# Two-layer hybrid encoder on one core: another order of work around the feed-forward part, down projection in chunks of 3, 4, 4 pairs

## Chip, cores, metric

The kernel runs on 1 core of one Trainium2 chip. The metric is the time of one execution on the device, in microseconds (us); of several runs the median is given.

## What is computed

The reference runs two layers over x (1 x 1024 x 1024, float32). Each layer mixes tokens (attention, a spatial gate and a short convolution side by side) and then applies a convolutional gated feed-forward part, which is where the change lies:

```python
h = _rmsnorm(x, norm1_g[l]); p = h @ w_in[l]
...
x = x + mix @ w_out[l]
h2 = _rmsnorm(x, norm2_g[l])
up = _dwconv3(h2 @ ffn_w_up[l], ffn_conv_w[l])      # 1024 -> 5632, 3 taps along the sequence
gate, val = jnp.split(up, 2, axis=-1)               # 2816 each
x = x + (jax.nn.silu(gate) * val) @ ffn_w_down[l]   # 2816 -> 1024
```

## The kernel before

One core goes through the layers one after the other. A layer is: norm1 and the input projection; attention with the spatial gate and the convolution woven in; the output projection (`out_proj`, matmuls of lines 132 to 134); norm2 (`norm_a`, line 229, and `norm2_b`, transposes of line 679); the up projection in NFF = 22 tiles (`up_tile`); and the down projection (`down_chunk`). The order of instructions on each engine is set by the framework's scheduler, which simulates a time line of its own and takes, per engine, what it thinks ready; only inside `manual_schedule` does an engine keep the order in which the code is written, and before the change that is done for TensorE during attention alone.

Float32 matmuls are done as three: every operand is split into a rounded high half and the remainder, the low half (`split`: ScalarE copies the high half, line 108; VectorE or GpSimd subtracts it, line 119, as a letter `v` or `p` says). A product a x b is then high x high, high x low, low x high.

Both projections of the feed-forward part use a scheme with seven products of half-size blocks instead of eight (with sums of blocks as operands).

- **Up projection.** The operands on the activation side, named 11, 12, S1 to S4 and 22, are made once per layer at the end of norm2. `norm2_b` forms them per block of 128 rows (lines 695 to 698: VectorE and GpSimd), and `norm2_end` splits S1 to S4 when all blocks are there. On the weight side each tile f loads 2 x 512 KB (`up_load`, line 729), forms T1 to T4 on GpSimd (`up_prep`, line 745) and splits all seven (`up_split`). A tile is 7 products of 12 matmuls of 128x512 (`block_mm`, line 768) into PSUM banks named pa, po and pf. VectorE adds them up (line 796) and ScalarE copies the rest (line 797), a depthwise convolution of 3 taps follows for value and gate (`conv3`: one step on ScalarE, line 352, two on VectorE, lines 353 and 357), in two double banks named `big`; then the gate: tanh (line 822), lines 823 and 828 or 831 on VectorE. After every second tile four sums of blocks are formed (line 838) and the pair's seven operands are stored to DRAM (`gdram`, lines 829 and 841). Two tiles' first two products are started early, during norm2 (`up_ahead`).
- **Down projection.** 11 pairs of tiles, in CHUNKS = (2, 3, 3, 3) pairs. A chunk runs over the seven products m = 0 to 6; for each pair the operands are loaded from `gdram` (line 884), the weights (loaded at line 864) are subtracted on GpSimd where the product wants it (line 877), and both are split (`down_split`) into a ring of DRING slots. The matmuls (line 920) go to four banks: those with even m accumulate in two `big` double banks over the whole chunk, those with odd m go to pa, pa, po, pf. VectorE adds the banks into x (line 930), at each m. With 12 matmuls per pair and product there are 11 x 7 x 12 = 924 per layer.

PSUM has two `big` (two banks each), two pa, one po and one pf: all eight banks. SBUF is cut into named slots (H0 to H5, E0 to E9, W0 to W5, G0 to G7, Z0, Z1); a slot can be refilled when all that reads it is done. H0 and H1 hold x in the down projection. The program's `run` (from line 946) sets the order: norm2 blocks in a loop from line 1015, the tiles from line 1030, the chunks from line 1042. Three lines say what sets the places of PSUM:

```python
U, G = [self.big(), self.big()], {}                     # line 904
banks = [U[h][:, lo], U[h][:, hi]]                      # m even, line 912
banks = [self.acc(k) for k in (("pa", "pa"), ("po", "pf"))[h]]   # m odd, line 914
```

Of the kernel before, what the change touches and what calls it, by code (L numbers as in the profile page):

```python
# [11 lines left out]
ALU = mybir.AluOpType  # L12
# [21 lines left out]
CHUNKS = (2, 3, 3, 3)  # L34
DW = (("E3", "E4", "E8", "W3"), ("H4", "E3", "E4"), ("H2", "E8", "W3"), ("H4", "E3", "E4"))
DA = ("H3", "H5")
DRING = (
    "W1", "W4", "Z0", "Z1", "G0", "G2", "G3", "W2", "E0", "E1", "E2", "E5", "E6", "E7", "E9",
    "G6", "G7", "W0", "W5", "G4", "G1", "G5",
)  # L40
D_LO = "vvp"
D_T = "p"
D_SUM = "vvvv"
UPRING = ("E0", "E1", "E2", "E5", "E6", "E7", "E9", "G6", "G7")
# [11 lines left out]
CWE = ("p", "p")  # L56


class Trunk:
# [657 lines left out]

    def a_op(self, n, k):
# [19 lines left out]

    def up_prep(self, f, raws, B):


        b11, b21, b12, b22 = raws

        def sub(out, a, b):
            self.nc.gpsimd.tensor_tensor(out=out, in0=a, in1=b, op=ALU.subtract)  # L745

        if not B:
            B["11"] = self.up_split(b11, "v")
        sub(b11, b12, b11)
        B["T1"] = self.up_split(b11)  # L750
        sub(b11, b22, b11)
        B["T2"] = self.up_split(b11, "v")
        if "21" not in B:
            B["21"] = self.up_split(b21)
        sub(b12, b22, b12)
        B["T3"] = self.up_split(b12, "v")
        B["22"] = self.up_split(b22)
        sub(b21, b21, b11)
        B["T4"] = self.up_split(b21)
# [13 lines left out]
    def up_ahead(self, f, raws):  # L773

        B = {"11": self.up_split(raws[0], "v"), "21": self.up_split(raws[1], "v")}
        u, c2 = self.acc("pa"), self.acc(("po", "pf")[f])
        self.block_mm(u, "11", B["11"], True, False)
        self.block_mm(c2, "12", B["21"], True, True)
        if f == 0:
# [3 lines left out]
        return B, u, c2, p1  # L783

    def up_tile(self, f, B, ahead=None):
# [315 lines left out]
```

## Time and profile before

| | |
|---|---|
| median of 3 runs | 2300.79 us (2300.1 to 2304.73) |
| the profiled execution | 2304.89 us, its span 2303.1 us |
| TensorE (PE): busy, instructions | 2222.9 us (97%), 10564 |
| VectorE (DVE) | 1657.6 us (72%), 2123 |
| ScalarE (ACT) | 1121.1 us (49%), 2009 |
| GpSimd (POOL) | 1287.6 us (56%), 1133 |
| mean granted TensorE clock | 0.984 |

The profile is one execution on the chip. Busy is the time in which an engine has an instruction; "idle before" is the time for which it had none, with the instruction whose end released it. The granted clock is 1 at TensorE's higher level (2.4 GHz) and about 0.5 at its lower one (1.2 GHz). A layer ends at about 1154 us (layer 0) and 2297 us (layer 1).

### The profile page before, as it was taken

What the parts mean: (1) busy time and instruction counts of PE and PEld (TensorE: products, weight loads), DVE (VectorE), ACT (ScalarE), POOL (GpSimd) and SP (SyncE); (2) the same over time, 40 slices, a digit from 0 to 9 for tenths busy, and PEclk for the clock granted to TensorE, in tenths of its full rate; (3) what the DMA queues carried; (4) which work ended last, traced back from release to release, by engine and by line L of the source; (5) the groups of instructions that cost most, each with busy time, mean ns of one, the idle gap of its engine ahead of it and who ended that gap; (6) DMA issues with size and microseconds to landing.
All of it is one profiled execution on the core that took longest, in us unless ns stands there. A gap on an engine that the chain in (4) does not pass through costs nothing.

```text
span 2303.1 us, 29303 instructions
## 1 busy us (share of the span) xinstructions
PE 2222.9 (97%) x10564; PEld 1840.9 (80%) x10564; DVE 1657.6 (72%) x2123; ACT 1121.1 (49%) x2009; POOL 1287.6 (56%) x1133
## 2 busy tenths in 40 slices
PE   7999999989999999799999999999899999988998
PEld 6887887868888888588878878878688888876887
DVE  5468887276777777988645688862767777779885
ACT  4246776354544444443242467754545444444431
POOL 5463335685555554776454533356765555556761
PEclk9999999999999999899999999999899999999999
DMA  5000003222232325843230000041223333357431
GB/s 183 23 28 10 10 10 95 98 83 87 92 115 92 115 92 175 304 156 106 67 122 6 28 10 10 10 163 48 74 87 101 110 105 105 105 190 268 152 96 74
DMA packets 166852, 218.97 MB, mean 95 GB/s; under 512 B 11799, under 2 KB 117811, under 8 KB 166707
## 3 DMA queue, kind: packets, MB, share of 16 engines
q1 hardware_dynamic: 166706, 217.10, 28.3%
q8 instruction: 83, 1.36, 0.2%
q14 instruction: 63, 0.51, 0.1%
HBM read 159.92 MB, written 57.15 MB: 94 GB/s over the span
## 4 chain that ended last, share of the span: by engine, by line
PE 89%; DVE 4%; POOL 2%; DMA 2%; ACT 1%; issue 1%; SPq 0%; DVEq 0%; POOLq 0%; ACTq 0%
PE pa L768 20%; PE big L920 10%; PE pf L768 9%; PE pf L266 5%; PE po L768 5%; PE pa L536 5%; PE pa L920 3%; PE pa L134 3%; PE pa L133 3%; PE big L520 3%; PE big L519 3%; PE pa L132 3%; PE po L548 2%; PE po L549 2%; PE pf L920 2%; PE po L920 2%
## 5 line engine op out<-in xcount | busy, mean ns | idle before, releaser
L528 POOL TENSOR_SCALAR H<-H,rv 128x1024 f32<-128x1024 f32 x128 | 144.8, 1131 | 272.2 <-DVE rv L527 272.2
L119 POOL TENSOR_TENSOR E<-E,E 128x512 fp32r<-128x512 f32 (+1 forms) x123 | 167.6, 1364 | 172.7 <-ACT E L108 172.2
L108 ACT ACTIVATE E<-E 128x512 fp32r<-128x512 f32 (+1 forms) x227 | 141.6, 629 | 182.0 <-POOL E L745 69.3
L768 PE MATMUL pa<-H,E 128*128 128x512 f32 x840 | 210.8, 395 | 12.3 <-DVE H L796 12.3
L541 DVE TENSOR_TENSOR E<-pa,E 128x512 fp32r<-128x512 f32 x256 | 173.4, 688 | 49.6 <-ACT E L540 48.2
L768 PEld LDWEIGHTS pa<-H,E 128*128 128x128 f32 x840 | 160.0, 191 | 46.7 <-DVE H L796 13.2
L540 ACT ACTIVATE E<-pa 128x512 fp32r<-128x512 f32 x256 | 152.9, 597 | 90.4 <-PE pa L536 89.2
L536 PEld LDWEIGHTS pa<-ident,H 128*128 128x128 f32 x1024 | 128.0, 141 | 42.8 <-issue 5.1
L536 PE MATMUL pa<-ident,H 128*128 128x128 f32 x1024 | 154.9, 274 | 6.6 <-DVE E L541 6.6
L522 DVE TENSOR_REDUCE nm<-big 128x1 f32<-128x1024 f32 x128 | 155.7, 1216 | 6.7 <-PE big L520 6.6
L353 DVE SCALAR_TENSOR_TENSOR big<-H,cst,big 128x1023 f32<-128x1023 f32 x44 | 56.6, 1287 | 143.8 <-ACT big L352 143.8
L797 ACT ACTIVATE H<-pa 128x512 f32<-128x512 f32 x128 | 76.0, 594 | 164.0 <-PE pa L768 148.0
L525 ACT ACTIVATE H<-big,nm 128x1024 f32<-128x1024 f32 x128 | 142.4, 1112 | 17.7 <-DVE nm L522 17.6
L119 DVE TENSOR_TENSOR E<-E,E 128x512 fp32r<-128x512 f32 (+1 forms) x109 | 117.9, 1084 | 24.1 <-ACT E L108 24.1
L266 PE MATMUL pf<-H,G 128*128 128x512 f32 x320 | 130.7, 429 | 2.7 <-DVE Z L394 2.7
L768 PE MATMUL pa<-W,E 128*128 128x512 f32 x340 | 119.2, 400 | 12.7 <-ACT W L108 12.7
L108 ACT ACTIVATE G<-E 128x512 fp32r<-128x512 f32 (+2 forms) x126 | 68.6, 556 | 106.1 <-PE pa L133 21.0
L745 POOL TENSOR_TENSOR E<-E 128x512 f32<-128x512 f32 x66 | 103.1, 1563 | 4.4
L768 PE MATMUL po<-H,E 128*128 128x512 f32 x408 | 104.6, 389 | 0.0
L548 PE MATMUL po<-E,E 128*128 128x512 f32 x256 | 101.5, 396 | 2.1 <-DVE E L564 2.1
L108 ACT ACTIVATE G<-H 128x512 fp32r<-128x512 f32 (+1 forms) x94 | 58.5, 649 | 90.7 <-PE big L920 43.7
L549 PE MATMUL po<-E,E 128*128 128x512 f32 x256 | 101.3, 396 | 0.0
(430 smaller groups left out, 6554.1 us busy)
## 6 DMA issues: line engine op xcount, KB each, us to landing
E<-in_ffn_w_up_dram SPq DMA_DIRECT2D x66, 512.0 KB
gdram<-H SPq DMA_DIRECT2D x66, 512.0 KB
H<-gdram SPq DMA_DIRECT2D x66, 512.0 KB
out_dram<-H SPq DMA_DIRECT2D x32, 512.0 KB
E<-in_w_in_dram SPq DMA_DIRECT2D x30, 512.0 KB
H<-out_dram SPq DMA_DIRECT2D x24, 512.0 KB
H<-in_ffn_w_down_dram SPq DMA_DIRECT2D x24, 512.0 KB
W<-in_ffn_w_up_dram SPq DMA_DIRECT2D x22, 512.0 KB
```

Source lines behind the costliest of these rows:

```text
L108: nc.scalar.activation(out, in_, AF.Copy)
L119: e.tensor_tensor(out=l, in0=src, in1=h.bitcast(F32), op=ALU.subtract)
L266: mm(acc, a[:, k, :], b, start=k + j == 0, stop=k == KC - 1 and j == 2)
L522: nc.vector.tensor_reduce(out=nm, in_=S, op=ALU.max, axis=AX.X, negate=True)
L528: nc.gpsimd.tensor_scalar(out=p, in0=p, scalar1=rv, scalar2=1.0, op0=ALU.mult, op1=ALU.mult)
L536: nc.tensor.transpose(pt[:, r * P : (r + 1) * P], pu[:, r, kc * P : (kc + 1) * P], self.ident)
L540: nc.scalar.activation(hl[:, 0, :], pt, AF.Copy)
L541: nc.vector.tensor_tensor(out=hl[:, 1, :], in0=pt, in1=hl[:, 0, :].bitcast(F32), op=ALU.subtract)
L548: self.nc.tensor.matmul(O, v, hl[:, 0, :], start=kc == 0, stop=False)
L549: self.nc.tensor.matmul(O, v, hl[:, 1, :], start=False, stop=kc == 7)
L768: mm(out, w, x, start=first and k + j == 0, stop=k == 3 and j == 2, skip_group_check=True,)
L920: nc.tensor.matmul(o, p, r, start=n + q == 0 and (m % 2 == 1 or m == 0), stop=n == len(ops) - 1 and q == 2, skip_group_check=True,)
```

## The change

1. The end of norm2 (blocks 6 and 7, `norm2_end`, and the weight operands of tiles 0 and 1) is written out in an order that VectorE, GpSimd and ScalarE must keep. Tile 0's weights and half of tile 1's are loaded when block 2 is done, and three of tile 0's operands are formed at block 4. S2 is split first, then S1 and S3, then S4, whose low halves both go to VectorE (one went to GpSimd). The first two tiles run the product S1 after S2.
2. In the last tile (f = 21), the down projection is begun (`down_begin`): the operands of product 0 of the first chunk are loaded and split, the subtractions for product 1 done and x is loaded, ahead of the tile's last products; the operands of product 1 are split between the steps of its convolution. The four sums at its end go to GpSimd. From there to the end of chunk 0 VectorE, GpSimd and ScalarE keep the written order (`FREE`).
3. The down projection has three chunks (3, 4 and 4 pairs). Products with even m accumulate in the banks pa, po, pa, pf over the whole chunk, those with odd m use `big`. Operands are formed and split one product ahead of the matmuls, the ring of slots has 18 entries for 22, and the slots of the weights are others. The first 12 low halves alternate GpSimd and VectorE, then v, v, p as before. With three chunks instead of four there are 21 products to be added into x per layer instead of 28.

The number and shape of matmuls is the same. The core of the diff:

```diff
-CHUNKS = (2, 3, 3, 3)
+CHUNKS = (3, 4, 4)
...
-DA = ("H3", "H5")
+DA = ("H5", "H3")
...
 D_LO = "vvp"
+FREE = (0, 6)
+D_LO0 = "pvpvpvpvpvpv"
...
+MANUAL = {mybir.EngineType.DVE, mybir.EngineType.Pool, mybir.EngineType.Activation}
...
+            ("S2", r1[:, 4:8], ("W1", "W4", "Z0", "Z1"), "vv"),
             ("S1", r0[:, 0:4], self.xo[1], "vv"),
-            ("S2", r1[:, 4:8], ("W1", "W4", "Z0", "Z1"), "vv"),
             ("S3", r1[:, 0:4], ("G0", "G2", "G3", "W2"), "vv"),
-            ("S4", r0[:, 4:8], ("W5", "G4", "G1", "G5"), "vp"),
+            ("S4", r0[:, 4:8], ("W5", "G4", "G1", "G5"), "vv"),
...
         add(uv[:, hi], u, p5)
+        if L is not None:
+            self.order = ExitStack()
+            self.order.enter_context(self.tc.manual_schedule(engines=MANUAL))
+            self.down_begin(L)
         self.block_mm(c5, "S4", B["22"], False, True)
...
-        cv, cg = self.big(), self.big()
+        cg, cv = self.big(), self.big()
+        self.conv3(cv, uv, scales(NFF + f))
+        if L is not None:
+            self.down_ops(0, 1, (0,))
+            cp(ug[:, hi], u)
+        self.conv3(cg, ug, scales(f))
+        if L is not None:
+            self.down_ops(0, 1, (1, 2))
...
-            self.vp(D_SUM[e]).tensor_tensor(out=o, in0=p, in1=q, op=op)
+            self.vp("p" if L is not None else D_SUM[e]).tensor_tensor(out=o, in0=p, in1=q, op=op)
...
+    def down_begin(self, L):
+        self.drn = self.dan = 0
+        self.ga = [self.slot(t, [4, 2, 512]) for t in DA]
+        self.dops = {}
+        self.down_ops(0, 0)
+        for b11, b12, _, _ in self.dW[0]:
+            self.vp(D_T).tensor_tensor(out=b11, in0=b12, in1=b11, op=ALU.subtract)
+        self.alloc_x(self.xreg)
+        xout = self.out[0].rearrange("(b p) d -> b p d", p=P)
+        for b in range(NB):
+            self.load_x(b, xout)
+    def down_step(self, c, m, store):
...
+        if m == 0:
+            self.dU = [self.acc(k) for k in ("pa", "po", "pa", "pf")]
+        ops = self.dops.pop((c, m))
+        for h in range(2):
+            if m % 2 == 0:
+                banks = self.dU[2 * h : 2 * h + 2]
+                parts = [(banks[j], 2 * h + j) for j in range(2)]
+            else:
+                bg = self.big()
...
+    def down(self, L, store):
+        steps = [(c, m) for c in range(len(CHUNKS)) for m in range(7)]
+        for n, (c, m) in enumerate(steps):
+            if n + 1 < len(steps) and steps[n + 1] not in self.dops:
+                self.down_ops(*steps[n + 1])
+            if m == 2 and c + 1 < len(CHUNKS):
+                self.down_w(L, c + 1)
+            self.down_step(c, m, store)
+            if (c, m) == FREE:
+                self.order.close()
...
+            for b in range(NB):
+                self.norm2_step(b, xs, g2, xout)
+                if b == 2:
+                    raws[0], raws[1] = self.up_load(L, 0), self.up_load(L, 1, (0,))
+                elif b == 4:
+                    self.up_prep(0, raws[0], ("11", "21", "T1", "t2", "t3", "t4"))
+            raws[1] += self.up_load(L, 1, (1,))
+            with self.tc.manual_schedule(engines=MANUAL):
+                xs[7] = self.norm_a(7, self.x[7], g2, ("G1", "G5"))
+                ahead.append(self.up_ahead(0, self.B[0]))
+                self.up_prep(1, raws[1], ("11", "21"))
+                self.norm2_b(6, xs[6])
...
+                self.norm2_b(7, xs[7])
...
+                self.norm2_end(("S2", "S1", "S3"))
...
+                self.norm2_end(("S4",))
+                self.up_prep(1, raws[1], ("T3", "22", "T4"))
```

**Order on VectorE at the end of norm2** (layer 0; names are the program's slots with a running number; H_904 holds raw S2 and S3, H_903 raw S1 and S4). Before:

```order
L696 TENSOR_TENSOR H_904_4409<-big_4913,H_904_4409 128x4x128
L119 TENSOR_TENSOR E_1005_5037<-W_979_4930,E_1005_5037 128x512
L119 TENSOR_TENSOR H_957_4798<-big_4965,H_957_4798 128x4x128
L695 TENSOR_TENSOR H_904_4409<-H_903_4408,big_4965 128x4x128
L696 TENSOR_TENSOR H_904_4409<-big_4965,H_904_4409 128x4x128
L119 TENSOR_TENSOR G_992_4995<-H_904_4409,G_990_4993 128x1024
L119 TENSOR_TENSOR W_993_4996<-H_904_4409,G_991_4994 128x1024
L119 TENSOR_TENSOR Z_988_4987<-H_904_4409,W_986_4985 128x1024
L119 TENSOR_TENSOR Z_989_4988<-H_904_4409,W_987_4986 128x1024
L119 TENSOR_TENSOR E_1004_5033<-E_978_4928,E_1004_5033 128x512
L119 TENSOR_TENSOR H_985_4980<-H_903_4408,H_985_4980 128x1024
L796 TENSOR_TENSOR H_1008_5047<-po_4878,W_972_4903 128x512
```

Now:

```order
L125 TENSOR_TENSOR E_983_4947<-E_925_4559,E_983_4947 128x512
L125 TENSOR_TENSOR H_963_4817<-big_4950,H_963_4817 128x4x128
L701 TENSOR_TENSOR H_904_4409<-H_903_4408,big_4950 128x4x128
L702 TENSOR_TENSOR H_904_4409<-big_4950,H_904_4409 128x4x128
L125 TENSOR_TENSOR G_985_4965<-E_926_4561,G_985_4965 128x512
L125 TENSOR_TENSOR Z_990_4997<-H_904_4409,W_988_4995 128x1024
L125 TENSOR_TENSOR Z_991_4998<-H_904_4409,W_989_4996 128x1024
L125 TENSOR_TENSOR H_992_5003<-H_903_4408,H_992_5003 128x1024 x2
L125 TENSOR_TENSOR G_995_5010<-H_904_4409,G_993_5008 128x1024
L125 TENSOR_TENSOR W_996_5011<-H_904_4409,G_994_5009 128x1024
L810 TENSOR_TENSOR H_1008_5050<-po_4899,W_982_4945 128x512
```

The lows of S2 (into Z0 and Z1) came third and fourth of the row, after S3's two, in the scheduler's order; now they come first, and the six lows of 128x1024 stand together.

**Order on TensorE in tile 21** (pa_7871 and pa_7886 take the last product, "22" with T4, from H and E; line 920, now 966, are the down projection's). Before:

```order
L768 MATMUL pa_7871<-G_991_4994,G_1292_7754 128x512
L768 MATMUL pa_7871<-H_957_4798,E_1294_7761 128x512 x12
L920 MATMUL pa_8059<-G_1321_8049,G_1320_8046 128x512 x2
L920 MATMUL po_8077<-G_1321_8049,G_1320_8046 128x512 x2
L920 MATMUL pf_8078<-G_1321_8049,G_1320_8046 128x512 x2
L920 MATMUL pa_8060<-G_1321_8049,G_1320_8046 128x512 x2
```

Now:

```order
L780 MATMUL pa_7886<-G_994_5009,G_1292_7757 128x512
L966 MATMUL pa_8054<-W_1313_7962,W_1312_7959 128x512
L966 MATMUL po_8055<-W_1313_7962,W_1312_7959 128x512
...
L966 MATMUL pa_8054<-G_1317_7976,G_1316_7973 128x512
L966 MATMUL po_8055<-G_1317_7976,G_1316_7973 128x512
L780 MATMUL pa_7886<-H_963_4817,E_1294_7764 128x512 x12
L966 MATMUL pa_8054<-G_1317_7976,G_1316_7973 128x512 x2
L966 MATMUL po_8055<-G_1317_7976,G_1316_7973 128x512 x2
L966 MATMUL pf_8057<-W_1313_7962,W_1312_7959 128x512 x3
...
L966 MATMUL big_8122<-W_1323_8025,G_1322_8022 128x512 x3
```

Fourteen matmuls of product 0 now stand ahead of the tile's last product, the other 22 behind it, and then product 1, into `big`.

**Order on VectorE in the same place** (H_1021 is tile 21's result; big_8017 and big_8018 its two convolutions). Before:

```order
L823 SCALAR_TENSOR_TENSOR H_1008_5047<-H_1008_5047,big_7859 128x1024
L119 TENSOR_TENSOR G_1347_8232<-H_1309_7994,G_1347_8232 128x512
L119 TENSOR_TENSOR G_1348_8235<-E_1311_7996,G_1348_8235 128x512
L828 TENSOR_TENSOR W_1300_7868<-big_7858,H_1008_5047 128x1024
L119 TENSOR_TENSOR W_1345_8200<-H_1309_7994,W_1345_8200 128x512
L796 TENSOR_TENSOR H_1021_5156<-pa_7871,H_1021_5156 128x512
```

Now:

```order
L125 TENSOR_TENSOR W_1313_7962<-E_1301_7874,W_1313_7962 128x512
L852 SCALAR_TENSOR_TENSOR H_1008_5050<-H_1008_5050,big_7861 128x1024
L125 TENSOR_TENSOR Z_1315_7969<-E_1303_7876,Z_1315_7969 128x512
L857 TENSOR_TENSOR W_1300_7871<-big_7862,H_1008_5050 128x1024
L810 TENSOR_TENSOR H_1021_5159<-pa_7886,H_1021_5159 128x512
L125 TENSOR_TENSOR G_1317_7976<-E_1305_7878,G_1317_7976 128x512
...
L125 TENSOR_TENSOR W_1323_8025<-E_1301_7874,W_1323_8025 128x512
...
L125 TENSOR_TENSOR G_1325_8035<-E_1303_7876,G_1325_8035 128x512
L125 TENSOR_TENSOR G_1327_8041<-E_1305_7878,G_1327_8041 128x512
L852 SCALAR_TENSOR_TENSOR H_1021_5159<-H_1021_5159,big_8017 128x1024
```

Between the gate of tile 20 and the add that reads pa stands one low where three stood; six lows, three each of products 0 and 1, stand ahead of the gate of tile 21, which reads the `big` bank.

## Rows read from the trace of the kernel before

**Rows 1.** The page: busy time per engine; granted TensorE clock in 40 slices, tenths.

```profile
PE 2222.9 (97%) x10564; PEld 1840.9 (80%) x10564; DVE 1657.6 (72%) x2123; ACT 1121.1 (49%) x2009; POOL 1287.6 (56%) x1133
...
PEclk9999999999999999899999999999899999999999
```

**Rows 2.** Waits of TensorE: line, what released it: us in total, times, longest.

```profile
PE pa L768 <- ACT W L108: 12.7, 2, 6.3
PE pa L768 <- DVE H L796: 12.3, 2, 6.9
...
PE pa L920 <- POOL G L119: 7.4, 2, 3.7
```

**Rows 3.** Windows: stretch, us, busy PE, PEld, DVE, ACT, POOL, clock, DMA share, GB/s.

```profile
580.00:910.00 330.00, 330.00 (x1458) 273.34 (x1457) 246.94 (x247) 159.99 (x242) 187.89 (x137) 1.00 0.33 106
...
935.00:1000.00 65.00, 58.29 (x241) 46.04 (x240) 63.17 (x69) 27.19 (x49) 44.37 (x29) 0.95 0.62 218
1000.00:1146.00 146.00, 146.00 (x646) 120.94 (x645) 117.61 (x132) 53.38 (x99) 90.30 (x63) 1.00 0.33 108
```

**Rows 4.** TensorE's timeline, end of norm2: start, us, what, [idle before, releaser].

```profile
491.05 3.01 PE L768 MATMUL pa<-H,E 128*128 128x512 f32 x12
...
500.33 1.06 PE L679 MATMUL big<-ident,G 128*128 128x128 f32 x8
501.15 3.34 PE L768 MATMUL pf<-H,E 128*128 128x512 f32 x12
...
515.21 0.80 PE L768 MATMUL pa<-Z,E 128*128 128x512 f32 x1 [3.60 <-DVE Z L119]
...
533.85 2.88 PE L768 MATMUL pa<-H,G 128*128 128x512 f32 x12
```

**Rows 5.** VectorE's timeline in the same stretch.

```profile
512.87 4.51 DVE L119 TENSOR_TENSOR Z<-H,W 128x1024 fp32r<-128x1024 f32 x2
517.30 1.76 DVE L119 TENSOR_TENSOR E<-E,E 128x512 fp32r<-128x512 f32 x1
...
522.33 0.68 DVE L796 TENSOR_TENSOR H<-po,W 128x512 f32<-128x512 f32 x1
```

**Rows 6.** TensorE's timeline, from the last up tile to layer 0's last product.

```profile
922.35 0.39 PE L768 MATMUL pa<-G,G 128*128 128x512 f32 x1
928.18 4.96 PE L768 MATMUL pa<-H,E 128*128 128x512 f32 x12 [5.44 <-DVE H L796]
...
939.61 0.80 PE L920 MATMUL pa<-G,G 128*128 128x512 f32 x1 [3.73 <-POOL G L119]
...
1153.38 0.85 PE L920 MATMUL big<-G,G 128*128 128x512 f32 x3
```

**Rows 7.** VectorE's timeline there.

```profile
921.70 1.20 DVE L823 SCALAR_TENSOR_TENSOR H<-H,big 128x1024 f32<-128x1024 f32 x1
...
930.80 1.28 DVE L353 SCALAR_TENSOR_TENSOR big<-H,csth,big 128x1023 f32<-128x1023 f32 x1
...
938.35 1.75 DVE L119 TENSOR_TENSOR E<-E,E 128x512 fp32r<-128x512 f32 x1
...
941.71 0.68 DVE L119 TENSOR_TENSOR G<-H,G 128x512 fp32r<-128x512 f32 x1
```

**Rows 8.** Groups of instructions, 1000 to 1146 us: busy us, mean ns, idle before.

```profile
L930 DVE TENSOR_TENSOR H<-big,H 128x1024 f32<-128x1024 f32 x20 | 24.3, 1216 | 11.0 <-PE big L920 11.0
L119 DVE TENSOR_TENSOR E<-H,E 128x512 fp32r<-128x512 f32 x17 | 18.3, 1097 | 2.9 <-ACT E L108 2.9
...
L877 POOL TENSOR_TENSOR H<-H 128x512 f32<-128x512 f32 x16 | 23.7, 1493 | 1.4 <-DMA H<-in_ffn_w_down_dram 0.6 <-DVE Z L119 0.6
```

**Rows 9.** TensorE's timeline, layer boundary and end of the program.

```profile
1158.46 1.97 PE L238 MATMUL big<-ident,Z 128*128 128x128 f32 x8 [3.15 <-DVE H L930]
1160.09 0.78 PE L132 MATMUL pf<-E,H 128*128 128x512 f32 x1
...
2296.08 0.84 PE L920 MATMUL big<-G,G 128*128 128x512 f32 x3
```

More of the change, by code (lines that the diff above doesn't have):

```diff
@@ L737, in up_split, with up_prep @@
         return t
-    def up_prep(self, f, raws, B):
+    def up_prep(self, f, raws, steps=("11", "T1", "T2", "21", "T3", "22", "T4")):
         b11, b21, b12, b22 = raws
[L744 to L759, printed above, removed]
+        B = self.B.setdefault(f, {})
+        of = {"11": b11, "T1": b11, "T2": b11, "21": b21, "T3": b12, "22": b22, "T4": b21}
+        subs = {"T1": (b12, b11), "T2": (b22, b11), "T3": (b22, b12), "T4": (b21, b11)}
+        for n in steps:
+            t = n.upper()
+            if t in subs and t not in self.formed.setdefault(f, set()):
+                p, q = subs[t]
+                self.formed[f].add(t)
+                self.nc.gpsimd.tensor_tensor(out=of[t], in0=p, in1=q, op=ALU.subtract)
+            if n == t:
+                early = f < 2 and n in ("11", "21")
+                B[n] = self.up_split(of[n], "v" if early or n in ("11", "T2", "T3") else "p")
     def block_mm(self, out, a, B, first, last):
@@ L782, in up_ahead, with up_tile @@
         self.nc.scalar.activation(p1, u, AF.Copy)
[L783 to L785 removed]
+        return u, c2, p1
+    def up_tile(self, f, B, ahead=None, L=None):
         nc = self.nc
@@ L804, in up_tile @@
             cp(p1, u)
-        self.block_mm(c5, "S1", B["T1"], True, False)
-        cp(p5, c5)
+        if not ahead:
+            self.block_mm(c5, "S1", B["T1"], True, False)
+            cp(p5, c5)
         self.block_mm(u, "S2", B["T2"], False, False)
         cp(u1, u)
+        if ahead:
+            self.block_mm(c5, "S1", B["T1"], True, False)
+            cp(p5, c5)
         if not ahead:
@@ L935, in down_chunk @@
-        return nxt
+        if m == 0:
[7 more added lines that the diff above has]
+                bg = self.big()
+                banks = [bg[:, lo], bg[:, hi]]
+                parts = [(bg.rearrange("p (j c) -> p j c", j=2), slice(2 * h, 2 * h + 2))]
+            for j, o in enumerate(banks):
+                s = slice((2 * h + j) * P, (2 * h + j + 1) * P)
+                for n, (a, b) in enumerate(ops):
+                    ah, al = a[:, 0, s], a[:, 1, s]
+                    for q, (p, r) in enumerate(((ah, b[:, 0]), (ah, b[:, 1]), (al, b[:, 0]))):
+                        nc.tensor.matmul(
+                            o, p, r, start=n + q == 0 and (m % 2 == 1 or m == 0),
+                            stop=n == len(ops) - 1 and q == 2, skip_group_check=True,
+                        )
+            for src, b in parts:
+                for d in dst[m]:
+                    nc.vector.tensor_tensor(out=d[:, b], in0=src, in1=d[:, b], op=ALU.add)
+            if c + 1 == len(CHUNKS) and store is not None and m >= 5:
+                for b in (2 * h, 2 * h + 1):
+                    b += 4 * (m - 5)
+                    nc.sync.dma_start(store[b], self.x[b])
@@ new lines, in run @@
+            for f in range(NFF):
+                if f > 0 and f + 1 < NFF:
+                    raws[f + 1] = self.up_load(L, f + 1)
+                    self.up_prep(f + 1, raws.pop(f + 1))
+                if f + 1 == NFF:
+                    self.dW, self.dG = {}, {}
+                    self.down_w(L, 0)
+                self.up_tile(
+                    f, self.B.pop(f), ahead[f] if f < 2 else None, L if f + 1 == NFF else None
+                )
+            self.down(L, xout if L == depth - 1 else None)
```

136 lines of the change are left out of this document (50 added, 86 removed).

## The prediction

> **What bounds the kernel now.** The page comes first: TensorE is busy 97% of the span, at full clock in nearly every slice [rows 1]. The change leaves the number of matmuls as it is, so it can win only where TensorE waits or runs at the lower clock; those places are looked for next. The list of TensorE's waits [rows 2] names two places where the change acts: the first tiles of the up projection (line 768, behind a split of line 108), and its last tile with the first products of the down projection (lines 768 and 920). Each wait occurs twice, once per layer, so one layer is worked out and doubled. A third is the boundary of the layers [rows 9]. The table by stage [rows 3] shows the rate: 1458 matmuls in 330.0 us in the middle of the up projection and 646 in 146.0 us in the steady down projection, that is 0.2263 us each, with TensorE never idle; from 935 to 1000 us it is busy 58.29 us of 65, at a mean granted clock of 0.95.
>
> From this rate follows what each transition loses. A: from the first block matmul at 491.05 to the end of the last product but one of tile 21 (922.35 plus one matmul, 922.58) [rows 4, 6] are 22 x 84 - 12 = 1836 matmuls, 415.5 us, and 16 transposes (8 take 0.82 us up to the next row), 1.6 us; 431.5 us passed, so **14.4 us** are lost. B: from there to 1154.06 (1153.38 plus three matmuls) [rows 6] are 12 + 924 matmuls, 211.8 us; 231.5 passed, **19.7 us** lost. C: the boundary between layers, 1154.06 to the first projection matmul at 1160.09 [rows 9], 6.0 us, once. D: the end, 2296.76 to 2303.1, 6.3 us, once [rows 9]. Over two layers some 80 us are there to be had.
>
> **Part A, the end of norm2.** VectorE paces it. Six low halves of 128x1024 follow each other at about 2.26 us (4.51 for two) [rows 5], and the first matmul that needs one starts at 515.21, when the third is done [rows 4]. The order was S1, S2, S3; the change puts S2 ahead, so its two lows stand where S1's two stood and the first is ready two lows earlier: 515.2 - 4.5 = 510.7. The last of the six moves less: a split of 1.76 and an add of 0.68 that stand between them [rows 5] go behind them, 2.4 us, and the norm of block 7 is written ahead of other work, which lets the six begin 1 to 3 us sooner. So the 72 matmuls of S1, S2 and S3 of both tiles, done at 533.85 now, come out done between 528.4 and 530.5: a gain of 3.4 to 5.4 us; I take **4 per layer**, and for the range 0 (the sixth low alone decides) and 14.4 (all of it).
>
> **Part B, the last up tile.** Now TensorE stands 5.44 us before the last product of tile 21 because VectorE's add (line 796), which has to read the bank first, stands behind three splits; then 3.73 us for a low on GpSimd, and the 12 matmuls after the first stop take 4.96 us instead of 2.72, at the lower level of the clock [rows 6]. The change does three things. It gives TensorE 36 matmuls of product 0 to do, some of them ahead of the last product: 48 matmuls are 10.9 us, 922.58 + 10.9 + 0.9 for short waits = 934.4, so the 5.44 goes. It splits operands a product ahead. And product 1 now goes into the `big` buffers, which hold tile 21's convolutions until the gate (line 852) has read them. That is **a new wait**, and what is late next. VectorE's row up to that gate, from its start at about 920.6 (durations from [rows 7]): six low halves, five at 1.66 (most at 1.75, some shorter) and one at 0.6, 8.9 us; three gate or product instructions of 1.2, which start 1.13 apart, 3.4; two adds, 1.3 (0.68 each, as in [rows 5]); four convolution steps at 1.28, 5.1; and 1.1 for ScalarE's step of the convolution: 19.8, so 940.4. TensorE, done at 934.4, waits **6.0**; then 2.2 us at the lower clock (4.96 - 2.72); about 1 for product 2, whose subtraction on GpSimd comes behind the four sums (line 867) moved there, and 1.3 for lows of products 3 and 4; with the 0.9 above, 11.4 us are still lost. Were all lows 0.68, the row would be 4.8 shorter and 6.6 lost; were all 1.75, the four sums on GpSimd too, and product 2 later by a subtraction, some 16. So B gives 19.7 - 11.4, **8 per layer** (3.5 to 13).
>
> Here row and rule bear on each other. The row: the same low split takes 0.68 at 941.71, when GpSimd has gone idle, and 1.75 at 938.35, beside it [rows 7]. The Trainium skill (SBUF — State Buffer, Who interferes with whom) says why: a VectorE instruction with both inputs in SBUF and a GpSimd one that reads SBUF take turns on one pair of ports, and the loser waits for the whole instruction. By the rule the lows stay long wherever GpSimd is kept busy, as the sums moved to it would keep it: B would then give the 3.5, and by the short row the 13. It is the mechanism of the first rival below.
>
> **Part C and D.** At the boundary both `big` buffers are free when product 6 ends, since it accumulates in the other banks, so the transposes of line 238 needn't wait for the last add: the 3.15 us there [rows 9] goes, less 0.6 for the smaller adds: **2.5**, once (0 to 4; part of the norm could come later, because its scratch slots Z0 and Z1 are used late in the ring of operands). At the end the last add is 128x512 and not 128x1024, 0.68 for 1.22 [rows 5, 8]: **0.5**, once.
>
> **The steady chunks.** Chunks of 4 pairs need 16 operand slots for two products, and 18 are there. VectorE per product of 4 pairs: 8 operands, of which two in three have their low on it, 5.33 at 1.06 (the mean over the stage, between 0.68 and 1.78; [rows 8] has a group at 1097 ns) plus 2.9 us of adds (four of 0.68, or two of 1.22; product 1 twice): 8.6. TensorE takes 48 x 0.2263 = 10.9. GpSimd: 2.67 lows at 1.49 and four subtractions in four of seven products: 7.4. All under 10.9, so TensorE covers it: **0**. Three chunks for four mean 28 - 21 = 7 products fewer of adds per layer, hidden behind TensorE already. Transfers: chunk 0's weights are loaded before the last up tile instead of after it, and x behind them; the DMA engines are busy 0.62 of 935 to 1000 us [rows 3], but none of TensorE's waits names a transfer [rows 2], so nothing for them.
>
> **Sum.** 2 x (4 + 8) + 2.5 + 0.5 = 27 us. The profiled execution took 2304.89 us (its span 2303.1 and 1.8 around it): 2277.9. It lies 4.1 above the median of the runs, 2300.79, against which the same 27 gives **2274**.
>
> **The rivals.**
> 1. Transitions stay bound by VectorE and GpSimd. For it: at 935 to 1000 us VectorE is busy 63.17 of 65 us [rows 3], and the change takes four sums from it but gives GpSimd them, beside which its lows are long. Against it: TensorE gets its filler whatever VectorE does. Then A gives 1 and B 3 per layer, C 2: 10 us, 2291.
> 2. Slower: chunks of 4 starve TensorE. If every low in the steady stage ran at 1.75 (all beside GpSimd), VectorE would need 5.33 x 1.75 + 2.9 = 12.2 per product against 10.9; over the 14 products of the two chunks of 4, both layers, 28 x 1.3 = 36 us, and the 27 gained are given back: 2301 - 27 + 36 = 2310. It decides once a product needs over 10.9 us, lows of 1.5 in the mean; now the mean is 1.06 [rows 8] with GpSimd busy 62% of the stage [rows 3], and the ring of 18 leaves only two operands to spare.
> 3. More is recovered: the lows become short, as at 941.71, and the waits of A and B vanish but for 9 us a layer: 2 x (34.1 - 9) = 50, 2251.
> 4. The change does not reach TensorE's order where it counts, or the new order is undone by a late operand of about equal price: 2300. The order listed ahead of this text shows the matmuls moved, so little is left for it.
>
> **How the numbers follow.** A measurement of this kernel can tell some 0.2%, 4.6 us, from no change: under 2296.2 is faster, over 2305.4 slower. Chances: my forecast 0.58 (its own range 2262 to 2288), rival 1 0.14, rival 2 0.12, rival 3 0.11, rival 4 0.05. Faster: the forecast, rival 3 and nearly all of rival 1, 0.82; same 0.06; slower 0.12. The range goes past the middle of rival 3, to 2246, and takes in rival 1, up to 2297; it leaves out rival 2, rival 4 and some of rival 3, together 0.2.
>
> **What would show it.** Right: no wait of TensorE for the add of tile 21 (up to 6.9 before), matmuls of the down projection before the last product of tile 21; a wait of 4 to 8 us for the gate before the first matmul into `big`; the third low of norm2's end some 4 us earlier; no wait on lows in the chunks of 4; the first projection matmul of layer 1 under 4 us after the last of the down projection. Wrong: a TensorE below 97% busy from chunk 1 on, a VectorE over 95% busy there, or waits on GpSimd's sums.

## The result and the profile after

The median is 2271.37 us (2268.49 to 2273.39, 4 runs) against 2302.76 us (2300.1 to 2305.08, 4 runs) of the kernel before: a ratio of 0.9866 with the 95% interval [0.9848, 0.9884], 31.4 us less. 2274 and a range of 2246 to 2297 had been forecast. The profiled execution took 2273.15 us, its span is 2271.3, so 31.8 us less than the span before.

The spans can be cut at the same places in both traces. A runs from the first block matmul to the end of product S3 of tile 21, B from there to the end of the layer's last down matmul, C to layer 1's first projection matmul, D from the last matmul to the end. "Start" and "middle" are what lies before A in layer 0 and between C and A of layer 1; the change does not touch them.

| us | start | A, layer 0 | B, layer 0 | C | middle | A, layer 1 | B, layer 1 | D |
|---|---|---|---|---|---|---|---|---|
| before | 491.1 | 431.5 | 231.5 | 6.0 | 472.7 | 432.0 | 231.9 | 6.4 |
| after | 489.7 | 426.5 | 223.1 | 5.4 | 471.9 | 426.4 | 223.9 | 4.5 |
| gain | 1.4 | 5.0 | 8.4 | 0.7 | 0.8 | 5.7 | 8.0 | 1.9 |
| forecast | 0 | 4 | 8 | 2.5 | 0 | 4 | 8 | 0.5 |

The page of the changed kernel (compare [rows 1]): as many matmuls, 7 us less busy time on TensorE, and no slice at 8 tenths of the clock.

```profile
PE 2216.0 (98%) x10564; PEld 1836.6 (81%) x10564; DVE 1634.0 (72%) x2065; ACT 1120.7 (49%) x2009; POOL 1300.9 (57%) x1143
...
PEclk9999999999999999999999999999999999999999
```

The list of TensorE's waits in the changed kernel (columns as in [rows 2]):

```profile
PE big L244 <- DVE Z L235: 12.1, 4, 7.8
PE big L966 <- DVE H L852: 8.2, 2, 4.3
PE pa L780 <- ACT H L811: 6.9, 2, 3.5
...
PE pa L780 <- DVE Z L125: 4.0, 4, 1.7
PE pa L966 <- DVE H L972: 3.0, 2, 1.5
PE pa L966 <- DVE G L125: 2.5, 4, 0.7
...
PE pa L780 <- ACT W L114: 0.3, 2, 0.2
```

Of the three waits of [rows 2] hardly anything is left: the 12.3 us for the add of tile 21 and the 7.4 for GpSimd's low are gone, and the 12.7 for ScalarE's high half is 0.3 in this list. In their place stand the gate (line 852, the new wait that was forecast), a copy of ScalarE (line 811, which was not), and adds of the down projection (line 972).

**Stretch A.** TensorE's timeline, layer 0 (as [rows 4]), and VectorE's (as [rows 5]):

```profile
489.70 2.99 PE L780 MATMUL pa<-H,E 128*128 128x512 f32 x12
...
502.83 0.50 PE L780 MATMUL pa<-W,E 128*128 128x512 f32 x1 [0.16 <-ACT W L114]
505.00 0.51 PE L780 MATMUL pa<-Z,E 128*128 128x512 f32 x1 [1.66 <-DVE Z L125]
...
514.65 3.21 PE L780 MATMUL pa<-G,G 128*128 128x512 f32 x7 [3.46 <-ACT H L811]
```

```profile
492.57 1.28 DVE L235 SCALAR_TENSOR_TENSOR G<-H,rsx,E 128x1024 f32<-128x1024 f32 x1
...
502.81 4.37 DVE L125 TENSOR_TENSOR Z<-H,W 128x1024 fp32r<-128x1024 f32 x2
507.11 2.35 DVE L125 TENSOR_TENSOR H<-H,H 128x1024 fp32r<-128x1024 f32 x2
509.38 2.30 DVE L125 TENSOR_TENSOR G<-H,G 128x1024 fp32r<-128x1024 f32 x1
511.60 2.28 DVE L125 TENSOR_TENSOR W<-H,G 128x1024 fp32r<-128x1024 f32 x1
```

The first matmul on a low of S2 comes 15.3 us after the first block matmul, before 24.2 [rows 4]. The six long lows end at 513.88. Then the copy of line 811 can run, for it writes into the slot from which S3 was being split, and TensorE, which had stood since 511.2, goes on.

Before, the largest wait of the stretch was another one, for the high half of S2 on ScalarE, ahead of the 3.60 us of [rows 4]:

```profile
510.81 0.80 PE L768 MATMUL pa<-W,E 128*128 128x512 f32 x1 [6.33 <-ACT W L108]
```

It is 0.16 us now (502.83). TensorE's idle time in stretch A falls from 9.9 us (6.33 + 3.60) to 5.6 (0.16 + 1.66 + 0.36 + 3.46), which is 4.3 of the 5.0 us gained in layer 0.

**Stretch B.** TensorE's timeline (as [rows 6]) and VectorE's (as [rows 7]):

```profile
915.99 0.39 PE L780 MATMUL pa<-G,G 128*128 128x512 f32 x1
916.22 0.39 PE L966 MATMUL pa<-W,W 128*128 128x512 f32 x1
...
919.39 2.88 PE L780 MATMUL pa<-H,E 128*128 128x512 f32 x12
...
926.41 0.84 PE L966 MATMUL pa<-G,G 128*128 128x512 f32 x3
931.18 1.54 PE L966 MATMUL big<-W,G 128*128 128x512 f32 x3 [3.93 <-DVE H L852]
932.52 1.49 PE L966 MATMUL big<-G,W 128*128 128x512 f32 x3
933.80 1.27 PE L966 MATMUL big<-G,G 128*128 128x512 f32 x3
934.91 0.85 PE L966 MATMUL big<-W,G 128*128 128x512 f32 x3
```

```profile
924.36 0.68 DVE L125 TENSOR_TENSOR W<-E,W 128x512 fp32r<-128x512 f32 x1
...
927.47 2.44 DVE L125 TENSOR_TENSOR G<-E,G 128x512 fp32r<-128x512 f32 x2
929.83 1.21 DVE L852 SCALAR_TENSOR_TENSOR H<-H,big 128x1024 f32<-128x1024 f32 x1
```

TensorE goes from the tile to the down projection without a stop, does the tile's last product unhindered at 919.39, and stops once product 0 is done, until the gate has read `big`. The nine matmuls after the stop take 3.73 us instead of the 2.04 of the steady rate; the granted clock from 931.2 to 934.9 is 0.54.

### The profile page after: what moved, and what is told of

It reads as the page before. It is cut to its first block, busy times and chain, and to the rows that moved or that the text cites. A ratio compares the mean times of both kernels' runs of the same rounds, so it can differ in the third digit from the quotient of the medians.

```text
span 2271.3 us, 29316 instructions
## 1 busy us (share of the span) xinstructions
PE 2216.0 (98%) x10564; PEld 1836.6 (81%) x10564; DVE 1634.0 (72%) x2065; ACT 1120.7 (49%) x2009; POOL 1300.9 (57%) x1143
## 3 DMA queue, kind: packets, MB, share of 16 engines
q8 instruction: 83, 1.36, 0.2%
## 4 chain that ended last, share of the span: by engine, by line
PE 86%; DVE 8%; DMA 3%; ACT 1%; issue 1%; POOL 0%; SPq 0%; DVEq 0%; ACTq 0%; POOLq 0%
PE pa L780 19%; PE pf L780 9%; PE big L966 6%; PE pf L272 5%; PE po L780 5%; PE pa L542 5%; PE pa L966 4%; PE pa L140 3%; PE pa L139 3%; PE pa L138 3%; PE big L526 3%; PE big L525 3%; PE po L554 2%; PE po L555 2%; PE po L966 2%; PE pf L966 2%
## 5 line engine op out<-in xcount | busy, mean ns | idle before, releaser
L114 ACT ACTIVATE E<-E 128x512 fp32r<-128x512 f32 (+1 forms) x217 | 135.5, 629 | 166.8 <-PE pa L780 50.4
L531 ACT ACTIVATE H<-big,nm 128x1024 f32<-128x1024 f32 x128 | 142.4, 1112 | 17.8 <-DVE nm L528 17.7
L114 ACT ACTIVATE G<-E 128x512 fp32r<-128x512 f32 (+2 forms) x148 | 82.3, 566 | 115.0 <-PE pa L139 21.0
L125 DVE TENSOR_TENSOR E<-E,E 128x512 fp32r<-128x512 f32 (+1 forms) x101 | 96.6, 964 | 23.2 <-ACT E L114 23.2
L125 DVE TENSOR_TENSOR G<-H,G 128x512 fp32r<-128x512 f32 (+1 forms) x78 | 104.3, 1349 | 9.4 <-ACT G L114 9.4
L125 POOL TENSOR_TENSOR G<-E,G 128x512 fp32r<-128x512 f32 x50 | 71.7, 1433 | 67.2 <-ACT G L114 67.2
```

Of the source, the lines that this page charges most:

```text
L114: nc.scalar.activation(out, in_, AF.Copy)
L125: e.tensor_tensor(out=l, in0=src, in1=h.bitcast(F32), op=ALU.subtract)
L531: nc.scalar.activation(p, S, AF.Exp, bias=nm, accum_out=sm)
```

## The experiments

All changes are made on the changed kernel, unless said otherwise. Line numbers in rows are those of each run's own kernel. The same cuts for every run, each from its one profiled execution (A0 is stretch A of layer 0, A1 that of layer 1, and so for B; medians are of 4 runs, of 10 for the last):

| us | median | A0 | A1 | B0 | B1 | C | middle | D |
|---|---|---|---|---|---|---|---|---|
| changed kernel | 2271.4 | 426.5 | 426.4 | 223.1 | 223.9 | 5.4 | 471.9 | 4.5 |
| a_undone | 2282.4 | 431.5 | 431.5 | 222.8 | 223.6 | 4.6 | 471.4 | 4.5 |
| a_free | 2282.2 | 432.2 | 430.8 | 223.0 | 223.9 | 4.6 | 470.7 | 4.5 |
| s_123 | 2268.1 | 425.1 | 424.4 | 222.4 | 223.9 | 5.4 | 472.5 | 4.5 |
| no_early | 2270.1 | 426.4 | 427.8 | 221.1 | 222.6 | 4.6 | 471.3 | 4.5 |
| sums_dve | 2267.6 | 425.0 | 426.5 | 221.5 | 222.3 | 4.6 | 469.4 | 4.5 |
| banks_old | 2287.8 | 426.6 | 426.3 | 224.9 | 226.5 | 13.2 | 472.9 | 6.4 |
| free_down | 2276.6 | 427.6 | 426.6 | 224.6 | 227.1 | 4.6 | 470.5 | 4.5 |
| chunks_3332 | 2274.2 | 426.5 | 426.4 | 223.6 | 222.1 | 7.3 | 473.0 | 6.1 |
| best1 | 2269.8 | 425.1 | 424.4 | 221.6 | 222.8 | 3.8 | 475.2 | 4.5 |
| best2 | 2279.7 | 427.1 | 427.0 | 222.5 | 222.7 | 3.7 | 473.2 | 4.5 |
| best3 | 2267.6 | 425.1 | 425.6 | 221.7 | 222.5 | 4.6 | 470.2 | 4.5 |
| before_banks | 2302.5 | 431.6 | 432.1 | 233.6 | 233.9 | 3.7 | 473.0 | 4.6 |

The middle, which no edit touches save the scratch of the two runs best1 and best2, differs by up to 3.6 us among the others (469.4 to 473.0), and the stretch before A by some 3. So an edit is judged by its own stretch, and totals only where they differ by more. The stretches spread too: among runs whose edit leaves A as in the changed kernel, A lies at 425.0 to 427.8; where it leaves B, B lies at 222.4 to 223.9; and C is 4.6 in most runs that don't touch it, 5.4 in the changed kernel and s_123. A difference of 1.5 us in a single run is at the edge of that and counts only where several runs agree.

**What carries A: three runs.** a_undone puts the whole end of norm2 back:

```diff
-            with self.tc.manual_schedule(engines=MANUAL):
-                xs[7] = self.norm_a(7, self.x[7], g2, ("G1", "G5"))
...
+            self.norm2_end(("S1", "S2", "S3", "S4"))
+            self.up_prep(0, raws[0], ("T1", "T2", "T3", "22", "T4"))
```

> The end of norm2 is put back to the order of before (scheduler's choice, S1 S2 S3 S4, weight operands formed late); last up tile and down projection stay as changed. Stretch A = first block matmul to the end of product S3 of tile 21 (426.5 and 426.4 us in the changed kernel, 431.5 and 432.0 before); stretch B = from there to the layer's last down matmul (223.1 and 223.9, before 231.5 and 231.9). Theory (A and B are independent, each part of the edit carries its own stretch): A back to 431 to 432.5 in both layers, B unchanged within 1 us, the time 10 us longer, about 2281. Rival (A's gain comes from the other slots and rings of the down part, not from the order): A stays under 428, time within 3 us of 2271.

A is back at 431.5 in both layers and B unmoved, as the theory has it: the two parts are independent. a_free keeps the program's new order but lets the scheduler decide:

```diff
-            with self.tc.manual_schedule(engines=MANUAL):
+            if True:
```

> The end of norm2 as changed (loads at block 2, operands of tile 0 at block 4, S2 first), but the scheduler orders VectorE, GpSimd and ScalarE. Theory (A's 5 us come from the operands of the first tiles being formed earlier, so that they don't stand among the six long lows): A within 1.5 us of 426.5 and 426.4. Rival (they come from the written order itself): A 429 to 432 in both layers, time 2276 to 2282.

The rival holds: 432.2 (just above its 432) and 430.8. The earlier loads and operands give nothing by themselves. The written order without them was not tried, so it is shown to be needed, not to be enough. VectorE's timeline of that run, and TensorE's:

```profile
497.92 2.30 DVE L235 SCALAR_TENSOR_TENSOR G<-H,rsx,E 128x1024 f32<-128x1024 f32 x1 [1.46 <-POOL rsx L133]
```

```profile
506.74 0.51 PE L780 MATMUL pa<-W,E 128*128 128x512 f32 x1 [3.00 <-ACT W L114]
512.43 0.79 PE L780 MATMUL pa<-W,E 128*128 128x512 f32 x1 [5.18 <-ACT E L114]
```

Block 7's norm is scaled 7.6 us after the first block matmul (497.92 - 490.37), by the written order after 2.9 (492.57 - 489.70), and TensorE waits for a weight operand of a tile that the scheduler split late. s_123 keeps the written order with S1 ahead of S2:

```diff
-            ("S2", r1[:, 4:8], ("W1", "W4", "Z0", "Z1"), "vv"),
             ("S1", r0[:, 0:4], self.xo[1], "vv"),
+            ("S2", r1[:, 4:8], ("W1", "W4", "Z0", "Z1"), "vv"),
```

> The hand order of norm2's end is kept, but S1 is split ahead of S2 (order S1, S2, S3, S4 as before the change). Theory of the prediction (S2 first lets the first matmul that needs a low start two lows earlier): A 3 to 4.5 us longer per layer, 429.5 to 431, time 2277 to 2280. Rival (the end of the stretch hangs on S3's lows: tile 0's first copy writes into the slot that raw S3 stands in, which is the wait of 3.46 us for line 811): A changes by less than 1.5 us, time 2269 to 2274.

A gets shorter, 1.4 and 2.0 us, so S2 first costs something. The rival was nearer (under 1.5 either way), with the second layer outside it and the time of 2268.1 just below its range. Two later runs with S1 first, best1 and best3, agree: the three have A at 424.4 to 425.6 (mean 425.0), the kernels with the changed kernel's order at 425.0 to 427.8 (mean 426.6), so S2 first costs some 1.6 us per layer. VectorE's six lows in s_123:

```profile
503.87 2.36 DVE L125 TENSOR_TENSOR H<-H,H 128x1024 fp32r<-128x1024 f32 x2 [2.24 <-ACT H L114]
...
509.56 2.31 DVE L125 TENSOR_TENSOR W<-H,G 128x1024 fp32r<-128x1024 f32 x1
```

From the first block matmul (488.61) they begin 2.2 us later than in the changed kernel and end 0.9 us sooner: they take 8.0 us for 11.1, since GpSimd, idle from 503.98 to 509.18, is out of their way for longer. In the changed kernel the two lows of S2 stand beside GpSimd's sums and take 4.37.

**What carries B.** no_early begins the down projection after tile 21 in the program:

```diff
-                    f, self.B.pop(f), ahead[f] if f < 2 else None, L if f + 1 == NFF else None
+                    f, self.B.pop(f), ahead[f] if f < 2 else None, None, f + 1 == NFF
                 )
+            self.order = ExitStack()
+            self.order.enter_context(self.tc.manual_schedule(engines=MANUAL))
+            self.down_begin(L)
+            self.down_ops(0, 1)
             self.down(L, xout if L == depth - 1 else None)
```

> The down projection is begun only after the whole of tile 21 (loads, splits and subtractions of product 0, the operands of product 1, in the same written order); banks, chunks, sums on GpSimd and operands a product ahead stay. Theory (matmuls of product 0 beside the last tile fill its waits): the wait before the last product of tile 21 is back at 3 to 6 us, stretch B 229 to 232 in both layers (+6 to +8 each), time 2283 to 2288. Rival (B's gain comes from the other banks and from operands a product ahead): B at most 226, time under 2277.

B is 2.0 and 1.3 us shorter, not longer. These numbers lie where the rival has them, but the run does not test it, for the edit did not undo what it was to undo: the order of TensorE and the tile itself are the scheduler's, and it put 21 matmuls of product 0 ahead of the tile's last product all the same (14 in the changed kernel). TensorE's timeline:

```profile
915.08 0.39 PE L966 MATMUL pa<-W,W 128*128 128x512 f32 x1
...
919.84 2.88 PE L780 MATMUL pa<-H,E 128*128 128x512 f32 x12
...
928.70 0.50 PE L966 MATMUL pa<-E,E 128*128 128x512 f32 x1 [2.55 <-ACT E L114]
...
936.88 0.86 PE L966 MATMUL big<-W,G 128*128 128x512 f32 x3
```

It also puts product 2 (into pa) ahead of product 1, so nothing waits for the gate. So the early call in the program is not what carries B; whether the matmuls beside the tile do, this run does not tell. banks_old takes this run and puts the roles of the PSUM banks back, which does keep them out:

```diff
-            self.dU = [self.acc(k) for k in ("pa", "po", "pa", "pf")]
+            self.dU = [self.big(), self.big()]
...
-            if m % 2 == 0:
+            if m % 2:
```

> Base: the run in which the down projection is begun after tile 21 in the program (stretch B 221.1 and 222.6 there, with 14 to 20 matmuls of product 0 ahead of the tile's last product all the same). The PSUM roles are put back as before the change: products with even m in the two big buffers, odd m in pa, pa, po, pf. Theory (B's gain is the swap of banks: product 0 finds its banks free while the big buffers still hold the convolution, so its matmuls stand beside the tile): no matmul of the down projection can run before the tile's last product, a wait of 3 to 6 us there is back, B 227 to 232 per layer, time 2278 to 2286. Rival (operands a product ahead and earlier loads carry it, whichever banks): B at most 224.5, time under 2274.

```profile
916.48 0.39 PE L780 MATMUL pa<-G,G 128*128 128x512 f32 x1
920.63 4.61 PE L780 MATMUL pa<-H,E 128*128 128x512 f32 x12 [3.76 <-DVE H L810]
...
1150.33 3.72 PE L244 MATMUL big<-ident,Z 128*128 128x128 f32 x16 [8.38 <-DVE Z L235]
```

The wait before the tile's last product is back, and B is 3.8 and 3.9 longer than in no_early, between both expectations. The banks are worth less than half of B here; but at the boundary C takes 13.2 for 4.6, and the end 6.4 for 4.5, neither of which was expected. In all the swap is worth 17.7 us of the median beside the rest of the change (2287.8 and 2270.1), about half of it at the boundary. free_down drops the written order from tile 21 on:

```diff
-            self.order.enter_context(self.tc.manual_schedule(engines=MANUAL))
```

> The changed kernel without the written order from the end of tile 21 through chunk 0: the scheduler orders VectorE, GpSimd and ScalarE there. Theory (banks carry B; the written order is worth little): B within 2 us of 223.1 and 223.9, time 2267 to 2275. Rival (the written order keeps lows that are wanted later from standing ahead of the add that TensorE waits for, as three did before the change): a wait of 3 us or more before the last product of tile 21 is back, B 226.5 to 231, time 2278 to 2287.

B is 1.5 and 3.2 longer, in layer 1 outside the first theory; the time of 2276.6 lies between the two ranges. The add before the tile's last product is no longer behind lows (0.4 us in one layer); instead TensorE waits later for product 2's high half, since the subtractions and lows of later products are mixed in. The waits from 905 to 1139 us of free_down:

```profile
PE pa L965 <- ACT E L114: 4.3, 1, 4.3
PE big L965 <- DVE H L851: 3.2, 1, 3.2
PE pa L965 <- POOL G L125: 1.0, 1, 1.0
```

before_banks does one part alone, on the kernel before: the swap of the banks (the diff is that of banks_old the other way round).

> The kernel before with one part of the change alone: products with even m in pa, po, pa, pf over the chunk, odd m in the two big buffers; chunks 2, 3, 3, 3, scheduler's order and everything else as before. Theory (the swap carries some 3.5 us of B per layer and about 2 us at the end, the rest hangs on operands formed a product ahead and on the written order): B 226 to 229.5 in both layers (231.5 and 231.9 before), end 4.3 to 5.3 us after the last matmul, time 2288 to 2297. Rival 1 (the swap alone carries B, the written order only mends what other edits spoil): B 222 to 225, time 2280 to 2288. Rival 2 (the swap alone is worth nothing, since the matmuls that it would let through have no operands yet): B 230.5 or more, time 2297 to 2304.

Rival 2 holds. The ratio is 1.0002 [0.999, 1.0013], B is even 2 us longer in both layers; C and D gain 2.3 and 1.8, which pays for it. TensorE's timeline:

```profile
925.71 5.02 PE L768 MATMUL pa<-H,E 128*128 128x512 f32 x12 [5.45 <-DVE H L796]
930.78 0.73 PE L921 MATMUL pa<-W,W 128*128 128x512 f32 x2
...
936.00 0.50 PE L921 MATMUL pa<-W,W 128*128 128x512 f32 x1 [3.57 <-DVE W L119]
```

The operands were the limit: the first of product 0 gets its high half on ScalarE only when the tile's last product is nearly done, and the low half that TensorE stops for comes after it:

```profile
930.11 0.62 ACT L108 ACTIVATE W<-H 128x512 fp32r<-128x512 f32 x1
```

Free banks without operands let nothing through. Beside the rest of the change (operands a product ahead, written order) the swap is worth 3.8 per layer in B; that rest without the swap brings B from 231.7 to 225.7 (means of the layers), with it to 221.8. How its 6 us divide between the operands formed ahead and the other edits was not tried apart.

**Sums and chunks.** sums_dve:

```diff
-            self.vp("p" if L is not None else D_SUM[e]).tensor_tensor(out=o, in0=p, in1=q, op=op)
+            self.vp(D_SUM[e]).tensor_tensor(out=o, in0=p, in1=q, op=op)
```

> The four sums at the end of tile 21 go back to VectorE. Theory (they don't matter: TensorE has product 1 to do when they run): B within 1.5 us of 223 to 224, time 2269 to 2274; the subtractions for product 2 on GpSimd start some 5 us earlier. Rival (the move to GpSimd relieved VectorE): the adds of product 0 come 3 to 7 us later behind four sums of 0.7 to 1.8 us, B 3 to 6 us longer per layer, time 2277 to 2283.

B is 1.5 and 1.6 shorter, at the edge of the theory; the time of 2267.6 is just below its range, and the rival (B longer) is out. A in layer 0 is 1.5 shorter as well, which the edit doesn't touch, so this run alone would not settle it; but best1 and best3, with the sums on VectorE too, have B at 221.6 to 222.8. The mean of the three is 222.1, that of the runs which leave B as in the changed kernel 223.3: the sums on GpSimd cost some 1.3 us per layer. GpSimd's first subtraction for product 2 in the changed kernel and in this run:

```profile
936.74 1.28 POOL L909 TENSOR_TENSOR E<-E,E 128x512 f32<-128x512 f32 x1
```

```profile
925.97 1.72 POOL L909 TENSOR_TENSOR E<-E,E 128x512 f32<-128x512 f32 x1
```

From the end of S3 (916.22 and 914.46) that is 20.5 and 11.5 us: behind the four sums it came 9 us later, and the waits for lows of products 2 to 4 are 0.9 us in two here and 1.8 in four there (layer 0). chunks_3332:

```diff
-CHUNKS = (3, 4, 4)
+CHUNKS = (3, 3, 3, 2)
```

> Four chunks (3, 3, 3, 2) for three (3, 4, 4) in the changed kernel, same ring of 18 slots, same matmuls; 28 products to add per layer for 21. Theory (VectorE needs some 8.6 us per product of 10.9 in chunks of 4, so the steady part is covered either way): B within 1 us of 223.1 and 223.9, no new wait of TensorE over 0.5 us after the first chunk, time 2268 to 2274. Rival (the added adds or the shorter products show): B 2 us or more longer per layer, time above 2275.

B is 0.5 longer and 1.8 shorter, with one wait of 0.7 us where none over 0.5 was expected: no cost of the seven more products to add. What the shorter last chunk loses, 2.0 in C and 1.7 in D, was not in the expectation.

**Putting the findings together.** best1 has S1 ahead of S2, the sums on VectorE, and other scratch slots at the boundary:

```diff
-                    xs[b] = self.norm_a(b, self.x[b], g1, ("Z0", "Z1"))
+                    xs[b] = self.norm_a(b, self.x[b], g1, ("G1", "G5") if L > 0 and b < 2 else ("Z0", "Z1"))
```

> Three edits on the changed kernel: S1 split ahead of S2, the four sums of tile 21 back on VectorE, and layer 1's first two norm blocks use G1 and G5 as scratch instead of Z0 and Z1, which the down projection's ring still holds for its last product. Theory (the three act in different stretches and add up): A 424 to 425.5 and B 221 to 223 as in the single runs, boundary C (last down matmul of layer 0 to first projection matmul of layer 1) 0.5 to 2.5 us for 5.4, time 2258 to 2264. Rival (C is set by the adds of product 6 and the transposes, not by Z0 and Z1): C stays at 4.5 us or more, time 2263 to 2268.

A and B come as expected, C does not (3.8), the middle is 3.3 longer than in the changed kernel, and the time of 2269.8 is above both ranges. VectorE's timeline at the boundary:

```profile
1130.82 4.53 DVE L235 SCALAR_TENSOR_TENSOR G<-H,rsx,W 128x1024 f32<-128x1024 f32 x2 [2.53 <-DMA W<-in_norm_g_dram]
```

With free slots the scaling waits for the next thing, the load of norm1's weights into W1, which the ring also holds late, and product 6's adds stand behind it. best2 orders S2, S3, S1 and begins the down projection after the tile:

> As the other run of this pair in the sums and the scratch, but with the down projection begun after tile 21 in the program, and the order S2, S3, S1. Theory (tile 0's first copy waits for S3's lows, so S3 ahead of S1 takes the wait of 3.46 us away): A 421.5 to 424 in both layers, B 220 to 222.5, C under 2.5, time 2254 to 2261. Rival (the six lows end at the same time in any order, and the work behind them with them): A 424.5 to 427, time 2260 to 2266.

```profile
511.23 2.93 PE L780 MATMUL big<-H,E 128*128 128x512 f32 x6 [3.02 <-DVE H L125]
```

The copy's wait went, and one of 3.02 us for S1's low came: the six lows end together whatever the order, as the rival has it (427.1 and 427.0, at the edge of it). The profiled execution is the fastest of the four (2270.6); the others took 2279.1 to 2280.7, and no row shows where they lost more. best3 keeps what held, S1 first and the sums on VectorE:

> Two edits on the changed kernel: S1 split ahead of S2, and the four sums of tile 21 back on VectorE; nothing at the boundary of the layers. Theory (the two act in different stretches and add up): A 424 to 425.5, B 221 to 222.8, boundary C 4.5 to 5.5, the stretch from there to layer 1's first block matmul 469 to 473 (475.2 in the run with the other scratch slots), time 2261 to 2267. Rival (what the single runs gained is only the spread of the parts that they don't touch): time 2268 to 2273 with A or B as in the changed kernel.

Its stretches are 5.0 us shorter than the changed kernel's (A 1.4 and 0.8, B 1.4 and 1.4), the ratio to before is 0.9845 [0.9827, 0.9864]. The median is 3.7 us lower, just above the expected range, and the intervals of the two ratios overlap: better by the stretches, not shown by the time alone.

## Why the prediction was right

- **The places** were right: 27.1 of the 31.8 us came in A and B, where 24 had been put. 2.2 came in stretches that the change leaves alone, which lies in their spread.
- **A: 4 per layer forecast, 5.0 and 5.7 measured.** The 4 was taken from the last of the six lows: 2.4 us for a split and an add that leave the row, 1 to 3 for an earlier start. Both came, and larger. From the first block matmul the lows began after 17.3 us before (508.38) and 13.1 now, and they take 11.1 us for 15.8, so the last one ends 8.9 us sooner. Only some of this reached A, because a wait that was not foreseen (3.46 us, line 811) stands behind it; and the largest wait of the stretch, the 6.33 us for S2's high half, was not priced at all, though it went. So the size is partly luck. S2 first did what was said at the first matmul on its lows (two lows sooner, though the two ahead of it had been S3's and not S1's), but the stretch did not hang on that matmul: by s_123, best1 and best3 it costs 1.6. Without the written order nothing of the gain is left (a_free).
- **B: 8 forecast, 8.4 and 8.0 measured.** The loss that stays was put at 11.4; it is 11.3 and 12.1. The wait for the gate came, at 3.9 and 4.3 for 6.0: the six lows ahead of it took 6.7 us (0.68 to 1.36 each), not 8.9. The stretch at the lower clock cost 1.7 for 2.2, the short waits 3.3 for 3.2; the rest, 2.4, mostly matmuls slowed around the waits, had been left out. The wait was put 2.1 too long and this 2.4 too short, so the total of 11.4 agrees partly by luck. That the matmuls beside the tile need both free banks and early operands was not separated in the prediction; banks_old and before_banks show it. How much of the rest the operands carry stays open.
- **The sums on GpSimd** were priced rightly as a delay of product 2 ("about 1"): taking them back gains 1.3.
- **C: 2.5 forecast, 0.7 measured** (1.4 by the runs with 4.6). Freeing `big` does let the 3.15 us of [rows 9] go: in before_banks, which has the banks and the old ring of slots, the transposes follow the last product at once and C gains 2.3. The step that failed is that nothing else would end later. In the changed kernel ScalarE's square of block 0 could start only at 1137.48, after product 6's last matmul on Z (busy until 1137.40); with other scratch, in best1, it ran at 1119.84. The row names an add of VectorE as releaser, which ended at 1137.45; but that add writes blocks 4 to 7, and in banks_old the same square is released by the matmul on Z. So the scratch was the limit, which the prediction had only as a remark for the range, and behind it the load of norm1's weights. The rows are those of the changed kernel, of banks_old and of before_banks:

```profile
1137.48 1.06 ACT L233 ACTIVATE Z<-H 128x1024 f32<-128x1024 f32 x1 [7.64 <-DVE H L972]
```

```profile
1139.77 1.06 ACT L233 ACTIVATE Z<-H 128x1024 f32<-128x1024 f32 x1 [7.63 <-PE big L966]
```

```profile
1153.91 1.91 PE L238 MATMUL big<-ident,Z 128*128 128x128 f32 x16
```

- **D: 0.5 forecast, 1.9 measured.** The add was 0.5 shorter. The rest goes with the banks (4.6 in before_banks, 6.4 in banks_old): the last add frees one block to store and no longer two. Not with the banks alone, though: chunks_3332 has them and 6.1, and there the last adds follow each other 1.4 us apart instead of 2.7. That the stores still under way make the difference is argued from this, not shown.
- **The steady chunks: 0 forecast,** one wait of 1.5 us per layer measured (line 972, at a change of chunk, where the banks kept over the chunk must be read first). VectorE is busy 117.0 of 145 us from 985 to 1130, 81%; 8.6 of 10.9 is 79%.
- **The rivals:** 1 (ports) didn't come about, since in stretch B GpSimd had gaps and the lows were shorter; 2 (starved chunks) neither, with no wait on a low after 965 us in layer 0; 3 neither. Of the signs named ahead one failed: layer 1's first projection matmul came 5.4 us after the last of the down projection, not under 4.

## What to carry to other kernels

Where a unit waits at a stage's border, ask for its next work's two conditions at once, a free place to write and a ready operand: in the last up tile the free banks alone gave nothing, with operands they gave 3.8 us per layer. Undo parts one by one even in a change that wins: two of its steps (S2 first, sums on GpSimd) cost some 1.6 and 1.3 us per layer under a gain of 13.5. And check on the engine's own order that an edit undid what it should: the early call could be taken out of the program and stayed in the machine.

## What the runs showed of the hardware

A low half of 128x1024 takes 1.2 us while GpSimd is idle and 2.2 to 2.3 beside it: the two at 507.11 took 2.35 together, those at 502.81 took 4.37. The rule that the prediction cited (the Trainium skill, SBUF — State Buffer, Who interferes with whom) agrees. After the stop of 3.93 us in stretch B TensorE ran some nine matmuls at its lower level (granted clock 0.54 from 931.2 to 934.9), 0.41 us each instead of 0.227: 1.7 us on top of the wait, almost half of its price again.
